# The first fifteen microseconds of a transformer layer: products of ones ahead of the first loads, x^T loaded in whole pairs, and a first contraction block in three rounds

## The chip, the cores and the metric

The kernel runs on one core of one Trainium2 chip. The metric is the device time in microseconds (us). The engines named here are TensorE (PE; its weight loads are shown as PEld), VectorE (DVE), ScalarE (ACT), GpSimd (POOL) and SyncE (SP), which issues nearly all loads and stores.

## The reference, cut to what matters

One layer over 1024 tokens of width 1024: two groups of attention heads side by side, cross-attention into 256 memory tokens, and a squared-ReLU MLP, each wrapped in RMSNorm. The change touches only the very first step, the input projection of the normalised x, and of it the values of the forgetting-attention heads:

```python
h = rmsnorm(x, g_mix_pre[l])
proj = h @ w_in[l]
fq = proj[..., 0:512]; fk = proj[..., 512:1024]; fv = proj[..., 1024:1536]
f_logit = proj[..., 1536:1544] + b_fgt[l]
...
x = x + rmsnorm(y @ w_out[l], g_mix_post[l])
...
x = x + rmsnorm(memory_cross_attention(...), g_mem_post[l])
...
x = x + rmsnorm(jnp.square(jax.nn.relu(h @ w_ff1[l])) @ w_ff2[l], g_ff_post[l])
```

All matrices are float32.

## The kernel before, in words

**Products.** A float32 product is made from three products in a faster form (fp32r): each operand is split into a high part (a rounded copy, made on ScalarE) and a low part (the rest, made on VectorE or GpSimd), and `mm3` (L172) issues high x high, high x low, low x high into the same PSUM bank. So no product can start before ScalarE has made the high parts of both operands, and the third waits for the low part of the activations.

**The opening (L1327 to L1495)** is written in the order in which it is to run; nothing is reordered by a planner there. It computes the values (`v`) of the forgetting heads for the first 512 tokens. x is not normalised first: x^T, scaled by the gain column `gp`, is split into `hT_hi` and `hT_lo` by `plain_split` (L1392, ScalarE at L1395, VectorE at L1396), and the row factor of the norm (`rall`, from squares of the rows of x) is applied when the banks are read out. The contraction over the 1024 features runs in eight blocks of 128 (kc = 0 to 7). `load_xt` (L1335) loads x^T in four pairs of blocks for each half of the tokens (tiles `xf`, 512 KB a pair), `load_wv` (L1341) loads the weights of the values (tiles `wv`; 264 columns in the first group, 256 in the second), and `wv_split` (L1374) makes `whiv` and `wlov` of them. The first pair and the first weight piece are cut in two, so that the first half pair (256 KB) and the weights of block 0 alone (132 KB) land first, and the two kinds are issued in turn (L1359):

```python
        for _ in zip(load_xt(0, 0, True), load_wv(0, 0, True)):
            pass
        list(load_xt(0, 1))
        list(load_wv(0, 1))
```

`value_part` (L1427) then goes block by block, and in a block bank by bank: four banks (128 tokens each), three products to a bank, 12 products of 264 columns to a block. Behind the 96 products of the first group come five blocks of the second group (60 products of 256 columns, needing low weights that GpSimd makes), then a small product `rt` (L1417) of a tile of ones with a diagonal of the row factors, then the other three blocks, and the same again for tokens 512 to 1023.

**Queues.** SP issues the loads one after the other, the gain column `gp` first (L1330). Each transfer signals on one of eight completion lanes in turn, and a transfer waits until the one eight places ahead of it has landed. ScalarE loads its table first, then waits for the weights of block 0. TensorE's first instruction is the first product of block 0. The constants (identity on GpSimd, two small columns and the tile `ones` on VectorE, L187 to L194) are written at the start; `ones` serves the products `rt`.

**The rest** (about 1420 us: attention, cross-attention and MLP) is recorded by a planner from estimated costs, which start at fixed numbers behind the opening and take no account of what stands in it.

Of the kernel before, what the change touches and what calls it, by code (L numbers as in the profile page):

```python
# [14 lines left out]
F32 = mybir.dt.float32  # L15
# [7 lines left out]
P = 128  # L23
S = 1024
D = 1024
KC = D // P
# [102 lines left out]
def layer(tc, out, t):  # L129
    nc = tc.nc  # L130
    ctx = ExitStack()
    with ctx:
        build(ctx, tc, nc, out, t)


def build(ctx, tc, nc, out, t):
    def pool(name, bufs=1, space=None, stack=ctx, **kw):
        if space is not None:
            kw["space"] = space
        return stack.enter_context(tc.tile_pool(name=name, bufs=bufs, reuse_waits="tile", **kw))  # L140

    const = pool("const")
# [7 lines left out]
    def mm_tile(shape, name, tag="mm"):  # L150
        return psp.tile(shape, F32, tag=tag, bufs=2, name=name)

    def u4(name, shape, dt=F32R):

        return up.tile(list(shape), dt, tag="u4", bufs=31, name=name)
# [16 lines left out]
    def mm3(ps, lh, ll, rh, rl, start, stop, more=False):  # L172

        nc.tensor.matmul(ps, lh, rh, start=start, stop=False, skip_group_check=more)  # L174
        nc.tensor.matmul(ps, lh, rl, start=False, stop=False, skip_group_check=more)  # L175
        nc.tensor.matmul(ps, ll, rh, start=False, stop=stop, skip_group_check=more)  # L176

    def rstd_of(ss, name):
# [5 lines left out]
        nc.gpsimd.tensor_tensor(r, r, mhalf[:, 0:1], op=ALU.pow)  # L184
        return r

    ident = const.tile([P, P], F32, name="ident")  # L187
    make_identity(nc, ident)
    mhalf = const.tile([P, 4], F32, name="mhalf")
    nc.vector.memset(mhalf, -0.5)  # L190
    o512 = const.tile([P, 1], F32, name="o512")
    nc.vector.memset(o512, 1.0 / 512.0)
    ones = const.tile([P, P], F32, name="ones")
    nc.vector.memset(ones, 1.0)  # L194
    bfgt = const.tile([P, 8], F32, name="bfgt")
    gcol = const.tile([P, KC], F32, name="gcol")
    gp = const.tile([P, KC], F32, name="gp")
# [1129 lines left out]
    stock = Stock()  # L1327
    back = Back()
    with tc.manual_schedule():
        nc.sync.dma_start(gp, t["g_pre"])  # L1330
        xf = [[None] * 4 for _ in range(2)]
        WV = ((0, 3), (3, 6), (6, 8)), ((0, 4), (4, 8))
        vraw = [[None] * 3, [None] * 2]

        def load_xt(th, kp, cut=False):  # L1335
            tag, n = (("klo", 4), ("sp", 5))[th]
            xf[th][kp] = p1.tile([P, 2, HT], F32, tag=tag, bufs=n, name=f"xf{th}{kp}")
            for c in (slice(0, 1), slice(1, 2)) if cut else (slice(0, 2),):
                yield nc.sync.dma_start(xf[th][kp][:, c, :], t["x_t"][th, kp][:, c, :])

        def load_wv(g, i, cut=False):  # L1341
            a, b = WV[g][i]
            shape = [P, b - a, 264 if g == 0 else 256]
            r = wp.tile(shape, F32, tag="wraw", bufs=3, name=f"wv{g}{i}") if g == 0 else u4(f"wv{g}{i}", shape, F32)
            vraw[g][i] = r
            for c in (slice(0, 1), slice(1, b - a)) if cut else (slice(0, b - a),):
                yield nc.sync.dma_start(r[:, c, :], t[f"w_v{g}"][:, a + c.start:a + c.stop, :])
# [8 lines left out]
            nc.sync.dma_start(r, t["x"][b * P:(b + 1) * P, :])  # L1356
            xrow.append(r)

        for _ in zip(load_xt(0, 0, True), load_wv(0, 0, True)):  # L1359
            pass  # L1360
        list(load_xt(0, 1))
        list(load_wv(0, 1))
        list(load_xt(0, 2))
        list(load_wv(0, 2))
        list(load_xt(0, 3))
        for i in range(2):
            list(load_wv(1, i))
        for b in range(4):
            load_row(b)
        for kp in range(4):  # L1370
            list(load_xt(1, kp))
        vs = [[u4(f"vs{g}_{i}", (P, 2, 4, P)) for i in range(4)] for g in range(2)]

        def wv_split(g, i, eng, cut=False):  # L1374
            raw = vraw[g][i]
            if g == 0:
                w = [u4(f"{m}v{g}{i}", raw.shape) for m in ("whi", "wlo")]
            else:
                w = [wp.tile(list(raw.shape), F32R, tag=m, bufs=2, name=f"{m}v{g}{i}") for m in ("whi", "wlo")]
            n = raw.shape[1]  # L1380

            def part(c):
                nc.scalar.activation(w[0][:, c, :], raw[:, c, :], AF.Copy)
                eng.tensor_sub(w[1][:, c, :], raw[:, c, :], f(w[0][:, c, :]))

            part(slice(0, 1 if cut else n))
            both = [(w[0][:, j, :], w[1][:, j, :]) for j in range(n)]
            return (both, lambda: part(slice(1, n))) if cut else both

        hT = [Act(f"hT{h}") for h in range(2)]  # L1390
# [31 lines left out]
        def value_banks(g, th):  # L1422
            tags = (("mm", "s"), ("tr", "pv"))[g]
            n = 264 if g == 0 else 256
            return [mm_tile([P, n], f"v{g}{th}{b}", tags[b // 2]) for b in range(4)]

        def value_part(banks, th, w, kcs):  # L1427
            for kc in kcs:
                for b in range(4):
                    c = slice(b * P, (b + 1) * P)  # L1430
                    mm3(banks[b], hT[th].hi(kc, c), hT[th].lo(kc, c), *w[kc], kc == 0, kc == KC - 1)
# [13 lines left out]
        w0, rest = wv_split(0, 0, nc.vector, True)  # L1445
# [8 lines left out]
        for kc in range(6, 8):  # L1454
            plain_split(0, kc)
        V = value_banks(0, 0)
        value_part(V, 0, w0, range(KC))
        w1 = wv_split(1, 0, nc.gpsimd)
        w1 += wv_split(1, 1, nc.gpsimd)
        for b in range(4):  # L1460
# [5 lines left out]
        stock.load(3)  # L1466
        W = value_banks(1, 0)
        value_part(W, 0, w1, range(5))
        d = root(0)
        values_out(0, 0, V)  # L1470
        spread(0, d, "s")
        value_part(W, 0, w1, range(5, 8))
        for kc in range(4):
            plain_split(1, kc)
        V = value_banks(0, 1)
# [64 lines left out]
    banks = [0]  # L1540

    def bank(name, tag=None):
        if tag is None:
            tag = ("mm", "s", "tr", "pv")[banks[0] % 4]
            banks[0] += 1
        return mm_tile([P, HT], name, tag)
# [54 lines left out]
    def first_row(j, wa, tags=(None, None)):  # L1601

        x = bank(f"px{j}", tags[0])
        product(x, wa, 0, B11)
        yb = bank(f"py{j}", tags[1])
        product(yb, wa, HT, B21)
        p1 = t2(f"p1_{j}")
        nc.scalar.activation(p1, x, AF.Copy)
        g11 = t2(f"g11_{j}")
        return x, p1, g11, lambda: nc.vector.tensor_add(g11, yb, p1)  # L1610
# [22 lines left out]
    xf = {}  # L1633
# [87 lines left out]
    for b in range(4):  # L1721
        c = slice(b * P, (b + 1) * P)
# [176 lines left out]
    with manual:  # L1899
        sums = lambda: None  # L1900
        for j in range(NP):
            more = j + 1 < NP
            after = Weights(j + 2) if j + 2 < NP else None
            w = cur.w
# [7 lines left out]
            if j < AHEAD:  # L1912
                p1, g11 = saved.pop(j)
                x = bank(f"px{j}")
            else:
                x, _, g11, add = first_row(j, w["a"])
# [156 lines left out]
        for n in range(7):  # L2073
# [4 lines left out]
            banks = Y if n in (1, 3, 5) else X  # L2078
# [87 lines left out]
```

## Time and profile before

| | |
|---|---|
| time, median of 3 runs | 1477.57 us (1474.86 to 1479.61) |
| time of the profiled execution | 1475.31 us |
| its span | 1473.5 us |
| PE busy | 1453.8 us (99%) |
| first product of block 0 | starts at 5.34 us |
| first product of block 1 | starts at 9.62 us |
| first product of the second group | starts at 22.11 us |

The span runs from the first instruction to the last in the profile; 1.8 us of the execution's own time lie around it. In the rows of the timeline the first number is the start in us from the start of the span, the second the duration; then engine, line, operation, output <- inputs, shape and count; in brackets stands the idle time before it and what ended that. Matmuls overlap in the rows: what one costs in a stream is the distance of the starts, not its duration.

### The profile page before, as it was taken

The numbers are of one execution on the slowest core, as the hardware profiler recorded it, in microseconds if no ns is written. First come the engines' busy times: TensorE is split into PE (matmuls) and PEld (weight loads), VectorE is DVE, ScalarE is ACT, GpSimd is POOL, SyncE is SP. The second block draws the span as 40 slices with busy tenths as digits, with TensorE's granted clock in tenths as the row PEclk, the third lists the DMA queues.
The fourth block names the chain that finished last, engine by engine and source line by source line (L and its number), as shares of the span: only waits on it lengthen the run. The fifth ranks groups of instructions, "written<-read, shape, count | busy, mean of one in ns | idle before, by whom it ended". The sixth has DMA issues, their size and how long they took to land. (4 is left out here: it accounts for less than half of the span.)

```text
span 1473.5 us, 20806 instructions
## 1 busy us (share of the span) xinstructions
PE 1453.8 (99%) x7260; PEld 1225.4 (83%) x7260; DVE 931.9 (63%) x1598; ACT 793.7 (54%) x1402; POOL 398.2 (27%) x488
## 2 busy tenths in 40 slices
PE   8999999999999999999999999999999999999998
PEld 7988888888889887888888887888888788888886
DVE  4467877667666545874474687765555666645577
ACT  6557776567577653554353455555555453444442
POOL 1335556444344201421121413342322000000021
PEclk9999999999999999999999999999999999999999
DMA  8234545635536677551341537764445785445565
GB/s 330 63 83 108 140 108 124 186 93 132 133 94 186 181 243 265 176 182 58 106 152 43 184 131 252 244 226 154 148 149 171 263 336 173 142 146 197 182 246 200
DMA packets 101753, 247.90 MB, mean 168 GB/s; under 512 B 12152, under 2 KB 24576, under 8 KB 101648
## 3 DMA queue, kind: packets, MB, share of 16 engines
q1 hardware_dynamic: 97040, 238.18, 48.5%
q0 software_dynamic: 4608, 8.39, 4.2%
q8 instruction: 57, 0.93, 0.3%
q14 instruction: 48, 0.39, 0.1%
HBM read 174.64 MB, written 71.88 MB: 167 GB/s over the span
## 5 line engine op out<-in xcount | busy, mean ns | idle before, releaser
L578 DVE TENSOR_TENSOR p<-ptr,p 128x512 fp32r<-128x512 f32 (+1 forms) x152 | 92.3, 616 | 40.9 <-ACT p L581 40.0
L1890 ACT ACTIVATE whif<-ra 128x1024 fp32r<-128x1024 f32 x37 | 39.2, 1061 | 122.7 <-PE fy L175 62.6
L1892 DVE TENSOR_TENSOR wlof<-ra,whif 128x1024 fp32r<-128x1024 f32 x37 | 45.3, 1225 | 91.7 <-ACT whif L1890 91.6
L581 ACT ACTIVATE p<-ptr 128x512 fp32r<-128x512 f32 (+1 forms) x152 | 79.6, 538 | 43.8 <-PE ptr L572 43.3
L2006 POOL TENSOR_SCALAR rf<-sf 128x1 f32<-128x1 f32 x8 | 8.2, 1031 | 326.7 <-ACT jf L1991 326.4
L622 PE MATMUL pv<-p,vs 128*128 128x512 f32 (+1 forms) x304 | 87.2, 373 | 1.7 <-DVE p L578 1.7
L174 PE MATMUL fx<-vhif,whif 128*128 128x512 f32 x168 | 65.4, 389 | 0.0
L175 PE MATMUL fx<-vlof,whif 128*128 128x512 f32 x168 | 65.4, 389 | 0.0
L176 PE MATMUL fx<-vhif,wlof 128*128 128x512 f32 x168 | 65.4, 389 | 0.0
L622 PEld LDWEIGHTS pv<-p,vs 128*128 128x128 f32 x304 | 53.4, 189 | 11.9 <-DVE p L578 3.5
L1780 POOL TENSOR_TENSOR sc<-wf,wf 128x512 f32<-128x512 f32 x14 | 22.4, 1597 | 142.7 <-DMA wf<-in_w_ff 134.7
L174 PE MATMUL k<-hT_hi,whik 128*128 128x512 f32 x128 | 52.7, 411 | 0.0
L174 PE MATMUL mq<-h2T_hi,whimq 128*128 128x512 f32 x128 | 51.6, 403 | 0.0
L174 PE MATMUL q<-hT_hi,whiq 128*128 128x512 f32 x128 | 51.1, 399 | 0.0
L174 PE MATMUL yw<-whiwo,yT_hi 128*128 128x512 f32 x128 | 50.8, 397 | 0.0
L631 ACT ACTIVATE ot<-pv 128x512 f32<-128x512 f32 x64 | 37.8, 591 | 23.5 <-PE pv L622 23.4
L174 PE MATMUL ym<-whimo,oT_hi 128*128 128x512 f32 x128 | 50.3, 394 | 0.1
L175 PE MATMUL k<-hT_lo,whik 128*128 128x512 f32 x128 | 50.2, 392 | 0.0
L176 PE MATMUL k<-hT_hi,wlok 128*128 128x512 f32 x128 | 50.2, 392 | 0.0
L175 PE MATMUL q<-hT_lo,whiq 128*128 128x512 f32 x128 | 50.1, 391 | 0.0
L175 PE MATMUL mq<-h2T_lo,whimq 128*128 128x512 f32 x128 | 50.0, 391 | 0.0
L176 PE MATMUL q<-hT_hi,wloq 128*128 128x512 f32 x128 | 50.0, 391 | 0.0
(592 smaller groups left out, 4928.5 us busy)
## 6 DMA issues: line engine op xcount, KB each, us to landing
ra<-gd SPq DMA_DIRECT2D x56, 512.0 KB, 3.8
wg<-in_w_ff SPq DMA_DIRECT2D x56, 512.0 KB, 5.1
wf<-in_w_ff SPq DMA_DIRECT2D x38, 512.0 KB, 3.8
gd<-s SPq DMA_DIRECT2D x48, 256.0 KB, 2.1
od<-ot SPq DMA_DIRECT2D x64, 128.0 KB, 2.4
od<-od POOLq DMA_DIRECT2D x32, 256.0 KB, 4.8
wrawmq<-in_w_mq SPq DMA_DIRECT2D x16, 512.0 KB, 4.1
wrawmo<-in_w_mo SPq DMA_DIRECT2D x16, 512.0 KB, 3.8
```

What stands on the lines that cost most here:

```text
L174: nc.tensor.matmul(ps, lh, rh, start=start, stop=False, skip_group_check=more)
L175: nc.tensor.matmul(ps, lh, rl, start=False, stop=False, skip_group_check=more)
L176: nc.tensor.matmul(ps, ll, rh, start=False, stop=stop, skip_group_check=more)
L578: flow.put("V", at, 0.56 if dead else 0.7, lambda: nc.vector.tensor_sub(pl[:, live, :], tr[:, live, :], f(ph[:, live, :])), done)
L581: flow.put("S", flow.end, 0.49 if dead else 0.6, lambda ph=ph, tr=tr, live=live: nc.scalar.activation(ph[:, live, :], tr[:, live, :], AF.C ...
L622: nc.tensor.matmul(pv[:, :, q0 * P:(q0 + k1 - k0) * P], v, x[:, :, k0:k1, :].rearrange("p m k q -> p m (k q)"), start=c == 0 and m == 0, s ...
L631: nc.scalar.activation(box["t"][:, :, :, ::step], pv.rearrange("p m (k q) -> p m k q", q=P), AF.Copy)
L1780: eng.tensor_sub(sc[:, k1], r0[:, k0], r1[:, k0])
L1890: nc.scalar.activation(ah, ra, AF.Copy)
L1892: nc.vector.tensor_sub(al, ra, f(ah))
L2006: nc.gpsimd.tensor_scalar(r, ssf[b][:, 0:1], ssf[b][:, 1:2], EPS, op0=ALU.add, op1=ALU.add)
```

## The change

- The tile `ones` is written first of all constants, so VectorE's first instruction is this memset.
- The gain column `gp` is loaded from ScalarE's queue, not from SP's.
- TensorE begins with seven plain float32 products of `ones` with `ones` (128 x 128 each) into a PSUM tile `warm` that nothing reads.
- The first pair of x^T is loaded as one transfer of 512 KB, not as two halves; the order of the first transfers is weights of block 0, first pair, rest of the first weight piece, and then as before.
- Block 0 runs in three rounds over the four banks: high x high for all four, then high x low weights for all four, then low x high for all four. Blocks 1 to 7 are as before.

```diff
@@ constants
+    ones = const.tile([P, P], F32, name="ones")
+    nc.vector.memset(ones, 1.0)
     ident = const.tile([P, P], F32, name="ident")
...
-    ones = const.tile([P, P], F32, name="ones")
-    nc.vector.memset(ones, 1.0)
@@ opening
-        nc.sync.dma_start(gp, t["g_pre"])
+        nc.scalar.dma_start(gp, t["g_pre"])
+        warm = mm_tile([P, P], "warm", "tr")
+        for _ in range(7):
+            nc.tensor.matmul(warm, ones, ones, start=True, stop=True)
...
-        def load_xt(th, kp, cut=False):
+        def load_xt(th, kp):
             tag, n = (("klo", 4), ("sp", 5))[th]
             xf[th][kp] = p1.tile([P, 2, HT], F32, tag=tag, bufs=n, name=f"xf{th}{kp}")
-            for c in (slice(0, 1), slice(1, 2)) if cut else (slice(0, 2),):
-                yield nc.sync.dma_start(xf[th][kp][:, c, :], t["x_t"][th, kp][:, c, :])
+            nc.sync.dma_start(xf[th][kp], t["x_t"][th, kp])
...
-        for _ in zip(load_xt(0, 0, True), load_wv(0, 0, True)):
-            pass
-        list(load_xt(0, 1))
+        first = load_wv(0, 0, True)
+        next(first)
+        load_xt(0, 0)
+        list(first)
+        load_xt(0, 1)
         list(load_wv(0, 1))
...
+        def value_first(banks, w):
+            hs, ls = ([x(0, slice(b * P, (b + 1) * P)) for b in range(4)] for x in (hT[0].hi, hT[0].lo))
+            for b in range(4):
+                nc.tensor.matmul(banks[b], hs[b], w[0], start=True, stop=False)
+            for b in range(4):
+                nc.tensor.matmul(banks[b], hs[b], w[1], start=False, stop=False)
+            for b in range(4):
+                nc.tensor.matmul(banks[b], ls[b], w[0], start=False, stop=False)
...
-        value_part(V, 0, w0, range(KC))
+        value_first(V, w0[0])
+        value_part(V, 0, w0, range(1, KC))
```

On TensorE's queue, at the very start of the program, the order before was this (`v` is a bank of the values, `hT_hi` and `hT_lo` the split x^T, `whiv` and `wlov` the split weights; in brackets the engine whose signal is waited for):

```order
L174 MATMUL v_230<-whiv_200,hT_hi_182 128x264 [waits Activation_49]
L175 MATMUL v_230<-wlov_201,hT_hi_182 128x264 [waits DVE_49]
L176 MATMUL v_230<-whiv_200,hT_lo_186 128x264 [waits DVE_49]
L174 MATMUL v_231<-whiv_200,hT_hi_182 128x264
L175 MATMUL v_231<-wlov_201,hT_hi_182 128x264
```

And with the change, at the same place:

```order
L1333 MATMUL warm<-ones 128x128 [waits DVE_49]
L1333 MATMUL warm<-ones 128x128 x6
L1434 MATMUL v_237<-whiv_207,hT_hi_189 128x264 [waits Activation_49]
L1434 MATMUL v_238<-whiv_207,hT_hi_189 128x264
L1434 MATMUL v_239<-whiv_207,hT_hi_189 128x264
L1434 MATMUL v_240<-whiv_207,hT_hi_189 128x264
L1436 MATMUL v_237<-wlov_208,hT_hi_189 128x264 [waits DVE_49]
L1436 MATMUL v_238<-wlov_208,hT_hi_189 128x264
L1436 MATMUL v_239<-wlov_208,hT_hi_189 128x264
L1436 MATMUL v_240<-wlov_208,hT_hi_189 128x264
L1438 MATMUL v_237<-whiv_207,hT_lo_193 128x264 [waits DVE_49]
```

The seven products stand in front of block 0 and wait for the memset alone; the wait for the low part of x^T moved from the third product of block 0 to the ninth.

SP's queue at the start of the program, before:

```order
L1330 DMA gp<-in_g_pre 128x8
L1339 DMA xf_138<-in_x_t 128x512
L1347 DMA wv_140<-in_w_v 128x264
L1339 DMA xf_138<-in_x_t 128x512
L1347 DMA wv_140<-in_w_v 128x528
L1339 DMA xf_144<-in_x_t 128x1024
L1347 DMA wv_146<-in_w_v 128x792
L1339 DMA xf_148<-in_x_t 128x1024
L1347 DMA wv_150<-in_w_v 128x528 [waits DMAHW0_49]
L1339 DMA xf_152<-in_x_t 128x1024 [waits DMAHW1_49]
```

And with the change (`DMAHW` are the eight completion lanes):

```order
L1349 DMA wv_146<-in_w_v 128x264
L1341 DMA xf_148<-in_x_t 128x1024
L1349 DMA wv_146<-in_w_v 128x528
L1341 DMA xf_151<-in_x_t 128x1024
L1349 DMA wv_153<-in_w_v 128x792
L1341 DMA xf_155<-in_x_t 128x1024
L1349 DMA wv_157<-in_w_v 128x528
L1341 DMA xf_159<-in_x_t 128x1024 [waits DMAHW0_49]
```

The weights of block 0 moved from the third place to the first and the rest of the first weight piece from the fifth to the third; everything behind stands two places earlier. `gp` still holds the first lane, now from ScalarE's queue, where it stands ahead of the table load. Behind block 0 the order of all five engines is the same in both kernels.

More of the change, by code (lines that the diff above doesn't have):

```diff
@@ L1357, in load_row @@
             xrow.append(r)
-        for _ in zip(load_xt(0, 0, True), load_wv(0, 0, True)):
-            pass
-        list(load_xt(0, 1))
+        first = load_wv(0, 0, True)
[3 more added lines that the diff above has]
+        load_xt(0, 1)
         list(load_wv(0, 1))
-        list(load_xt(0, 2))
+        load_xt(0, 2)
         list(load_wv(0, 2))
-        list(load_xt(0, 3))
+        load_xt(0, 3)
         for i in range(2):
@@ L1370, in build @@
         for kp in range(4):
-            list(load_xt(1, kp))
+            load_xt(1, kp)
         vs = [[u4(f"vs{g}_{i}", (P, 2, 4, P)) for i in range(4)] for g in range(2)]
```

## The prediction

> **What bounds the kernel now.** I read the page first, then the opening in the timeline, since the change touches nothing behind it.
>
> ```profile
> span 1473.5 us, 20806 instructions
> PE 1453.8 (99%) x7260; PEld 1225.4 (83%) x7260; DVE 931.9 (63%) x1598; ACT 793.7 (54%) x1402; POOL 398.2 (27%) x488
> ```
>
> TensorE bounds the whole: 19.7 us of the span are without a product. What the opening saves reaches the end if no load or side engine further on is late for an earlier TensorE. So the questions are how early TensorE's stream can run, and at what pace. Its start, products and ScalarE together:
>
> ```profile
> 0.73 1.28 ACT L1383 ACT_TABLE_LOAD   x1 [0.73 <-PEq L2159]
> 0.89 0.17 DVE L194 MEMSET ones<- 128x128 f32 x1
> 4.25 0.42 ACT L1383 ACTIVATE whiv<-wv 128x264 fp32r<-128x264 f32 x1 [2.25 <-DMA wv<-in_w_v]
> 4.58 0.71 ACT L1395 ACTIVATE hT_hi<-xf,gp 128x512 fp32r<-128x512 f32 x1
> 5.34 0.59 PE L174 MATMUL v<-whiv,hT_hi 128*128 128x264 f32 x1 [5.34 <-ACT hT_hi L1395]
> 6.13 0.59 PE L176 MATMUL v<-whiv,hT_lo 128*128 128x264 f32 x1
> 8.28 0.42 PE L176 MATMUL v<-whiv,hT_lo 128*128 128x264 f32 x1
> 8.31 0.64 ACT L1383 ACTIVATE whiv<-wv 128x528 fp32r<-128x528 f32 x1 [3.03 <-DMA wv<-in_w_v]
> 9.62 0.59 PE L174 MATMUL v<-whiv,hT_hi 128*128 128x264 f32 x1 [0.93 <-ACT hT_hi L1395]
> ```
>
> Block 0 runs from 5.34 to about 8.5 (last start 8.28 plus one distance). Block 1 waits until 9.62 for a load: the rest of the first weight piece comes at 8.3, ScalarE splits it, then x^T of block 1. So whatever block 0 saves on its own is spent waiting for block 1; only what moves 9.62, or the pace behind it, counts. The pace:
>
> ```profile
> 13.44 0.42 PE L174 MATMUL v<-whiv,hT_hi 128*128 128x264 f32 x1
> 13.66 0.42 PE L175 MATMUL v<-wlov,hT_hi 128*128 128x264 f32 x1
> 14.10 0.30 PE L174 MATMUL v<-whiv,hT_hi 128*128 128x264 f32 x1
> 14.48 0.28 PE L174 MATMUL v<-whiv,hT_hi 128*128 128x264 f32 x1
> 14.61 0.28 PE L175 MATMUL v<-wlov,hT_hi 128*128 128x264 f32 x1
> 22.11 0.28 PE L174 MATMUL v<-whiv,hT_hi 128*128 128x256 f32 x1
> ```
>
> Starts are 0.22 us apart up to 14.1 and 0.12 to 0.13 after it: TensorE ran at half pace until then (the granted-clock column still reads 1.00 there, so I go by the distances). From 9.62 to 14.10 stand 19 starts; at 0.12 they take 2.3 us, not 4.5. So the half pace costs at most 2.2 us behind 9.62. It ended after 4.5 us without an idle stretch; the 3.2 us of block 0, followed by 1.1 us idle, had not ended it. How fast it comes back shows at the kernel's end, where TensorE stops at about 1466.2:
>
> ```profile
> 1466.00:1468.00 2.00, 0.17 (x1) 0.00 (x0) 1.51 (x3) 0.72 (x2) 0.19 (x1) 1.00 0.68 262
> 1468.00:1470.00 2.00, 0.00 (x0) 0.00 (x0) 1.23 (x2) 0.00 (x0) 0.65 (x2) 0.55 0.00 0
> ```
>
> (Columns: busy time of PE, PEld, DVE, ACT, POOL, then granted clock, DMA share, GB/s.) A mean of 0.55 over 2 us means full clock for 0.2 us and half for the rest: the half clock is back at 1468.2, 2.0 us after the last product.
>
> **The change, part by part.** *Loads.* What SP issues first, and what the transfers reach:
>
> ```profile
> 0.73 0.39 SPq L1330 DMA_DIRECT2D gp<-in_g_pre  x1
> 1.17 0.42 SPq L1339 DMA_DIRECT2D xf<-in_x_t  x1
> 1.64 0.42 SPq L1347 DMA_DIRECT2D wv<-in_w_v  x1
> 2.58 0.43 SPq L1347 DMA_DIRECT2D wv<-in_w_v  x1
> 2.00:3.00 1.00, 0.00 (x0) 0.00 (x0) 0.00 (x0) 0.01 (x1) 0.00 (x0) 1.00 0.65 168
> 3.00:4.00 1.00, 0.00 (x0) 0.00 (x0) 0.00 (x0) 0.00 (x0) 0.00 (x0) 1.00 0.95 258
> 4.00:5.00 1.00, 0.00 (x0) 0.00 (x0) 0.29 (x1) 0.75 (x2) 0.00 (x0) 1.00 0.83 175
> 5.00:6.00 1.00, 0.66 (x2) 0.50 (x2) 0.82 (x2) 0.29 (x1) 0.00 (x0) 1.00 0.89 273
> 9.00:10.00 1.00, 0.38 (x1) 0.38 (x2) 1.00 (x2) 1.00 (x2) 0.00 (x0) 1.00 1.02 415
> ```
>
> SP issues one transfer per 0.47 us. Block 0's weights move from 1.64 to 0.73, the rest of that piece (block 1's) from 2.58 to 1.67, and everything behind stands 0.9 earlier, two issues fewer. The first bulk transfer is issued 0.44 earlier (1.17 to 0.73). That is the sure part; the other half of the 0.9 counts only where the DMA engines have room, and they are 65 to 95% busy from 2 us on. So block 1's data come between 0.44 and 0.92 earlier; I take 0.7, the middle, because neither end has a row nearer to it. If ready weights were no earlier at all, the term is 0. From 6 us on the loads are a stream at full rate, so the later ones shift by the same.
>
> `gp` on ScalarE's queue costs ScalarE one issue (0.39) ahead of the 1.28 table load: that ends at 2.4 instead of 2.0. ScalarE idles until 4.25 there, so it costs nothing; if the first weights land at 3.3 (2.6 after their issue, as before) 0.9 of cover is still left.
>
> *The whole first pair.* Block 0 now needs 512 + 132 KB instead of 256 + 132. The added 256 KB at 168 to 258 GB/s take 1.0 to 1.6 us, less the 0.44: x^T lands 0.6 to 1.2 later, around 4.9 to 5.5 if it was there at 4.3. First product at 5.9 to 6.5, not 5.34. Block 0 then takes 12 x 0.22 = 2.6 us at half pace and ends at 8.5 to 9.1. Block 1 is ready at 9.62 - 0.7 = 8.9. So this costs 0 to 0.2; the old wait ahead of block 1 is its cover.
>
> *Three rounds.* The two waits inside block 0 (its first three products take 1.18 us from 5.34 to 6.52, where three distances are 0.66) go, 0.5 us. Again in the shadow of block 1: worth nothing.
>
> *Memset.* `ones` first on VectorE: 0.17 us, the other two columns 0.17 later, used much later. Nothing.
>
> *Seven products of ones.* Their price is not in the trace of before. The nearest row is the `rt` product, also plain float32 and with ones as an operand, 512 columns, recorded as two instructions:
>
> ```profile
> 29.30 1.02 PE L1417 MATMUL rt<-diag,ones 128*128 128x512 f32 x2
> 16.05 4.88 POOL L1384 TENSOR_TENSOR wlov<-wv,whiv 128x1024 fp32r<-128x1024 f32 x2 [14.76 <-ACT whiv L1383]
> 23.89 0.87 DVE L1412 TENSOR_SCALAR diag<-ident,rall 128x128 f32<-128x128 f32 x4 [7.59 <-POOL rall L1409]
> 12.29 2.07 DVE L1396 SCALAR_TENSOR_TENSOR hT_lo<-xf,gp,hT_hi 128x512 fp32r<-128x512 f32 x3
> ```
>
> A quarter of its columns is 0.26 at full pace, 0.5 at half, so seven take 3.6 us, from about 1.1 (memset at 0.80 + 0.17, plus the signal) to 4.7. Upper end: if weight loads don't overlap, 14 instructions of 0.29 + 0.26 take 7.7 us and end at 8.8. They add nothing to TensorE's path as long as they end before 5.9; beyond that block 0 is pushed back.
>
> What they buy is pace. Busy stretches become 1.1 to 4.7 and 5.9 to 8.5, against 5.3 to 8.5 before. If the half pace ends in there and stays ended, block 1 on runs at 0.12. Its data allow nearly that: 12 products take 1.44 us, and the low parts of blocks 3 to 5 (12.29, three in 2.07) come 0.7 apart; block 3's is ready at 13.0 where the faster stream would use it at 12.74 (9.62 + 2 x 1.44 + 0.24), a wait of 0.3. So the gain behind block 1 is at most 2.2 - 0.3 = 1.9. The lower end is a full pace that comes no earlier relative to block 1: 0. I take 1.6, nearer the upper end: 6 us of work in the 7.4 us ahead of block 1 is more than the 3.2 in 4.3 that did not do it.
>
> [...]
>
> *Who is late next.* With 2.3 us gained the second group starts at 19.8 instead of 22.11. It needs GpSimd's first low weights, half of 4.88 after 16.05, so 18.5, itself moved earlier with its load. The `rt` product moves from 29.30 to 27.0; its diagonal is ready at 24.76. No wait. Behind it everything is relative to TensorE.
>
> **Sum.** 0.7 (loads) + 1.6 (pace) = 2.3 us off the profiled 1475.31, which gives 1473.0. The median of the runs lies 2.26 above the profiled execution; 2.3 off 1477.57 gives 1475.3, my forecast.
>
> **Rivals.** (1) *The products of ones don't change the pace.* They stop at 4.7, x^T comes at 5.9; the gap of over a second breaks the activity, as the 1.1 us gap did before. Then only the loads' 0.7 stays: 1476.9. For it speaks that 3.2 us did not suffice; against it that 3.6 and 2.6 us stand close together.
>
> (2) *The load start speeds up too.* From 2 to 6 us the loads moved 0.87 MB (168 + 258 + 175 + 273 GB/s), at the later 415 it would be 1.66 MB: 1.9 us are lost there. If whole pairs in longer rows cure that, block 1 comes 1.9 + 0.44 earlier, and with the pace 1.9: 4.2 us, 1473.3. Against it: the change only merges two of the first six transfers.
>
> (3) *Slower: the whole pair lands late.* All later loads share the engines with it, and a pair issued among seven others took 7.8 us:
>
> ```profile
> xf<-in_x_t SPq DMA_DIRECT2D x1, 512.0 KB, 7.8
> ```
>
> It decides once block 0 would end after 9.62 at half pace: landing + 0.71 + 2.64 > 9.62, a landing after 6.3, which is 5.1 after its issue at 1.2. At 7.8 it lands at 9.0, block 0 starts at 9.7 and ends at 12.3 with block 1 waiting behind: 2.7 us lost, 1480.3. Against it: the half pair took under 3.1 us (issue 1.17, in use at 4.58).
>
> **Chances.** The forecast 0.50; (1) 0.25; (2) 0.15; (3) 0.10. The forecast's own range is 1473.5 to 1477, from 0.5 to 4 us of gain, since the windows of the pace and 2 to 3 us of spread between runs are in it. The range for 8 in 10 goes from 1471.5 (case 2 and a low run) to 1479.2 (a third of the way into case 3, and a high run of no gain). About 0.3%, 4.4 us, is what a measurement of this kernel can tell from no change: faster means under 1473.1, slower over 1482.0. Under 1473.1 lie about half of (2) and a fifth of the forecast: 0.18. Over 1482.0 lies only a bad (3) in a high run: 0.06. Within: 0.76.
>
> **What would show it.** Right: seven products from about 1.1 to 4.7; the rest of the first weight piece split by ScalarE at about 7.6; block 1 at about 8.9; starts 0.12 apart from there on; the second group at about 19.8; `rt` at about 27.0, with no wait of TensorE ahead of it. Rival 1: starts 0.22 apart until after 12. Rival 2: over 350 GB/s from 3 us on. Rival 3: ScalarE waits for x^T past 6.3. The forecast is wrong if a place behind the opening changes by itself, or if the wait between blocks 0 and 1 brings the half pace back.

## The result

Over 14 runs of each kernel side by side the median went from 1474.88 us (1472.13 to 1479.61) to 1471.43 us (1469.61 to 1475.03). The ratio is 0.9978, with a 95% interval of 0.9969 to 0.9987: 3.2 us faster, between 1.9 and 4.6. The forecast was a gain of 2.3 from a median of 1477.57; the longer row of runs puts the kernel before 2.7 lower than the three runs did, and the time after lies 0.07 below the range stated for 8 in 10, and 2.1 below the forecast's own 1473.5 to 1477, for that reason. The gain itself was forecast 0.9 too small; it lies inside the 0.5 to 4 us that the forecast's own range stood for.

The page of the kernel after, and its opening in the timeline (columns as before: start, duration, engine, line, operation):

```profile
span 1467.8 us, 20832 instructions
PE 1453.2 (99%) x7274; PEld 1225.7 (84%) x7274; DVE 929.8 (63%) x1598; ACT 794.1 (54%) x1402; POOL 401.7 (27%) x488
```

```profile
1.05 3.35 PE L1333 MATMUL warm<-ones 128*128 128x128 f32 x14 [1.05 <-DVE o L194]
3.13 0.42 ACT L1387 ACTIVATE whiv<-wv 128x264 fp32r<-128x264 f32 x1 [0.69 <-DMA wv<-in_w_v]
4.89 0.72 ACT L1399 ACTIVATE hT_hi<-xf,gp 128x512 fp32r<-128x512 f32 x1 [1.33 <-DMA xf<-in_x_t]
5.52 0.63 ACT L1387 ACTIVATE whiv<-wv 128x528 fp32r<-128x528 f32 x1
5.66 0.76 PE L1434 MATMUL v<-whiv,hT_hi 128*128 128x264 f32 x4 [1.26 <-ACT hT_hi L1399]
7.23 0.29 PE L174 MATMUL v<-whiv,hT_hi 128*128 128x264 f32 x1
7.35 0.28 PE L175 MATMUL v<-wlov,hT_hi 128*128 128x264 f32 x1
7.73 0.39 PE L176 MATMUL v<-whiv,hT_lo 128*128 128x264 f32 x1
8.97 0.87 ACT L1387 ACTIVATE whiv<-wv 128x792 fp32r<-128x792 f32 x1 [0.32 <-DMA wv<-in_w_v]
9.17 0.28 PE L175 MATMUL v<-wlov,hT_hi 128*128 128x264 f32 x1
9.49 0.39 PE L176 MATMUL v<-whiv,hT_lo 128*128 128x264 f32 x1
10.92 0.37 PE L175 MATMUL v<-wlov,hT_hi 128*128 128x264 f32 x1
11.57 0.39 PE L176 MATMUL v<-whiv,hT_lo 128*128 128x264 f32 x1 [0.27 <-DVE hT_lo L1400]
18.69 0.28 PE L174 MATMUL v<-whiv,hT_hi 128*128 128x256 f32 x1
25.88 1.02 PE L1421 MATMUL rt<-diag,ones 128*128 128x512 f32 x2
```

The weights of blocks 3 to 5 were split in the kernel before at:

```profile
10.49 0.86 ACT L1383 ACTIVATE whiv<-wv 128x792 fp32r<-128x792 f32 x1 [0.26 <-DMA wv<-in_w_v]
```

The seven products of ones last from 1.05 to 4.40, and the full pace is there from block 0 on (four products from 5.66 in 0.76). The rest of the first weight piece, for which block 1 had waited until 8.31, is split at 5.52 with no wait for its load at all, 2.8 earlier; the weights of blocks 3 to 5 are split only 1.5 earlier (8.97). Block 1 starts at 7.23 instead of 9.62, the second group at 18.69 instead of 22.11, the `rt` product at 25.88 instead of 29.30. From there the two timelines run 3.4 to 3.5 us apart as far as 430 us. TensorE now waits inside blocks 1 to 3 for low parts of x^T (the products at 7.73, 9.49 and 11.57 start 0.38, 0.32 and 0.65 after the one ahead of them instead of 0.12): about 1 us. The last of these waits, at 11.57, ends a chain through ScalarE and VectorE that begins with the load of the weights of blocks 3 to 5 (8.97); behind it TensorE runs without a wait to the second group.

The loads by stages of 1 us (busy time of PE, PEld, DVE, ACT, POOL, then granted clock, DMA share, GB/s):

```profile
2.00:3.00 1.00, 1.00 (x7) 1.00 (x6) 0.00 (x0) 0.44 (x1) 0.00 (x0) 1.00 1.00 265
3.00:4.00 1.00, 1.00 (x7) 1.00 (x6) 0.41 (x1) 0.42 (x1) 0.00 (x0) 1.00 0.93 361
4.00:5.00 1.00, 0.40 (x2) 0.11 (x1) 0.02 (x1) 0.11 (x1) 0.00 (x0) 1.00 1.04 331
5.00:6.00 1.00, 0.34 (x2) 0.34 (x3) 0.36 (x1) 1.00 (x2) 0.00 (x0) 1.00 0.92 287
```

From 2 to 6 us the loads moved 1.24 MB, against 0.87 before.

The spans of the two profiled executions differ by 5.7 us, more than the medians. The 2.3 behind 430 us are not shown to be part of the change: TensorE's order is the same there, and three waits in each profile between 430 and 580 us, 2.6 us together before and 1.1 after, make 1.5 of it. They are, before and then after (engine, line and what it waited for: us, times, longest):

```profile
PE ptr L572 <- POOL spc6g L515: 1.1, 1, 1.1
PE pv L622 <- DVE p L578: 1.0, 1, 1.0
PE mv L174 <- ACT whimv L311: 0.5, 1, 0.5
```

```profile
PE sc6g L499 <- DVE mnc6g L503: 0.4, 1, 0.4
PE pv L622 <- DVE p L578: 0.4, 1, 0.4
PE mv L174 <- ACT whimv L311: 0.3, 1, 0.3
```

Such waits differ between two profiles of one and the same program: TensorE's idle time from 555 to 562 us, where the last one falls, was 1.05 in this profile of the changed kernel and 1.83 in its repetition (experiment 7).

### The profile page after: what moved, and what is told of

Same layout as the page of the kernel before. It is cut to its first block, busy times and chain, and to the rows that moved or that the text cites. A ratio compares the mean times of both kernels' runs of the same rounds, so it can differ in the third digit from the quotient of the medians.

```text
span 1467.8 us, 20832 instructions
## 1 busy us (share of the span) xinstructions
PE 1453.2 (99%) x7274; PEld 1225.7 (84%) x7274; DVE 929.8 (63%) x1598; ACT 794.1 (54%) x1402; POOL 401.7 (27%) x488
```

## The experiments

Theory at this point: the gain is made of earlier loads, which start block 1 earlier, and of the earlier full pace. Rivals: the loads alone, since the faster stream meets its data anyway; the ones alone; and luck of one run with the first loads. This table gathers what the profiles of all kernels show, so that the parts below need not repeat it; all times in us from the start of the span, read from the timelines as above ("rest split": when ScalarE starts on the rest of the first weight piece; "full pace": from when starts are 0.12 apart).

| kernel | x^T split | rest split | block 0 | block 1 | full pace | second group |
|---|---|---|---|---|---|---|
| before | 4.58 | 8.31 | 5.34 | 9.62 | 14.1 | 22.11 |
| after | 4.89 | 5.52 | 5.66 | 7.23 | from block 0 | 18.69 |
| after, once more | 5.08 | 5.71 | 5.85 | 8.66 | 8.8 | 18.88 |
| no ones | 5.12 | 5.75 | 5.90 | 8.71 | 11.2 | 20.01 |
| old loads | 4.51 | 8.07 | 5.28 | 9.38 | 13.5 | 21.68 |
| gain column on SP | 5.59 | 6.22 | 6.37 | 8.43 | from block 0, lost 7.3 to 10.7 | 19.62 |
| pair in halves, 2 KB rows | 3.83 | 7.32 | 4.60 | 8.62 | in block 0, lost 8.7 to 12 | 20.63 |
| pair in halves, 4 KB rows | 6.35 | 6.97 | 7.12 | 9.93 | 12.0 | 21.04 |
| pair ahead of the weights | 5.05 | 7.25 | 5.81 | 8.61 | 8.8 | 19.38 |
| no rounds | 5.63 | 6.26 | 6.41 | 9.56 | 12.3 | 20.98 |
| twelve ones | 4.90 | 5.55 | 5.68 | 7.23 | from block 0 | 18.69 |
| twelve ones, no rounds | 5.46 | 6.08 | 6.23 | 8.33 | from block 0 | 18.53 |
| twelve ones, all rounds | 5.04 | 5.67 | 5.82 | 7.38 | from block 0 | 17.95 |
| the same, and low weights last in mv | 5.37 | 6.00 | 6.19 | 7.73 | from block 0 | 17.99 |

**1. Without the products of ones.**

```diff
-        warm = mm_tile([P, P], "warm", "tr")
-        for _ in range(7):
-            nc.tensor.matmul(warm, ones, ones, start=True, stop=True)
```

> The changed kernel without the seven products of ones; loads and rounds as changed. Theory P (pace and loads both count): block 1 starts at about 7.5 to 8.5, its products stand 0.22 apart until a stretch of some 4 us without idle time has passed (until 10 to 13 us), the second group starts 1 to 2.2 us later than in the changed kernel (18.69), at 19.7 to 20.9; time between the two kernels. Theory L (the loads alone carry the gain, TensorE catches up with the data anyway): second group at 18.7 to 19.2. Theory O (the ones carry it all): second group at about 22.

The ratio to the kernel before is 0.9983 (0.9970 to 0.9997). In the profile the loads are as early as after the change, the pace is not; the products around its change:

```profile
10.91 0.42 PE L175 MATMUL v<-wlov,hT_hi 128*128 128x264 f32 x1
11.13 0.33 PE L176 MATMUL v<-whiv,hT_lo 128*128 128x264 f32 x1
11.30 0.28 PE L174 MATMUL v<-whiv,hT_hi 128*128 128x264 f32 x1
20.01 0.28 PE L174 MATMUL v<-whiv,hT_hi 128*128 128x256 f32 x1
```

Second group at 20.01: of the 3.4 us of the changed profile 2.1 came without any product of ones, 1.3 did not. That is what P expected (its block 1, at 8.71, came 0.2 past the 8.5: with block 0 at half pace it starts when block 0 is through; the half pace ended 5.3 us behind the start of block 0, with no idle time in between). It is one profile of each kernel, and the 2.1 hold more than earlier data: the half pace ended at 11.2 there and at 14.1 in the kernel before, where TensorE stood idle for about 1 us between blocks 0 and 1; here it did not. In the times the difference to the changed kernel is not resolved (0.9983 against 0.9978, intervals that overlap).

**2. The loads as before, ones and rounds kept.**

```diff
-        nc.scalar.dma_start(gp, t["g_pre"])
+        nc.sync.dma_start(gp, t["g_pre"])
...
-        first = load_wv(0, 0, True)
-        next(first)
-        load_xt(0, 0)
-        list(first)
+        first = load_wv(0, 0, True)
+        load_xt(0, 0)
+        for c, _ in zip((slice(0, 1), slice(1, 2)), range(2)):
+            nc.sync.dma_start(xf[0][0][:, c, :], t["x_t"][0, 0][:, c, :])
+            next(first)
```

(`load_xt` issues nothing for the first pair here.)

> The seven products of ones and the three rounds kept; gain column on SP first and the first pair in two halves in turn with the weights, as before. Theory P: block 1 back at about 9.6, products 0.12 apart if the full pace outlasts the idle time between blocks 0 and 1 (some 2.5 us), second group at 19.9 to 20.5 (the 1.9 us of the prediction's pace term gained, the rest lost). If the half pace comes back in that idle time: starts 0.22 apart again after 9.6 and second group at 21 to 22. Theory L: second group at about 22. Theory V (the early start of block 1 in the changed profile was one run's luck with the first loads): block 1 starts anywhere between 7 and 10 whatever the order of the loads.

The ratio is 1.0001 (0.9985 to 1.0016): no gain in the time. The profile:

```profile
1.05 3.35 PE L1333 MATMUL warm<-ones 128*128 128x128 f32 x14 [1.05 <-DVE o L194]
5.28 1.25 PE L1436 MATMUL v<-whiv,hT_hi 128*128 128x264 f32 x4 [0.87 <-ACT hT_hi L1401]
8.07 0.64 ACT L1389 ACTIVATE whiv<-wv 128x528 fp32r<-128x528 f32 x1 [2.85 <-DMA wv<-in_w_v]
9.38 0.59 PE L174 MATMUL v<-whiv,hT_hi 128*128 128x264 f32 x1 [1.10 <-ACT hT_hi L1401]
13.42 0.33 PE L175 MATMUL v<-wlov,hT_hi 128*128 128x264 f32 x1
21.68 0.28 PE L174 MATMUL v<-whiv,hT_hi 128*128 128x256 f32 x1
```

ScalarE waits for the rest of the piece until 8.07, as before the change; so the early loads are the work of the change and not luck, and V falls: the split comes at 8.07 and 8.31 in the two profiles with the old loads, and at 5.52 to 6.26 in the eight with the changed ones (one of them with another edit far behind). And although the seven products ran, block 0 ran at half pace (1.25 for four products), and the full pace came only at 13.5: the ones did nothing in this run. The expectation had taken the full pace in block 0 for granted; that was wrong. So this profile does not show what an early full pace would be worth with the old loads; the time says only that seven products of ones bring no gain there that is resolved, and twelve were not tried with them.

**3. The gain column first on SP's queue, the rest as changed.**

```diff
-        nc.scalar.dma_start(gp, t["g_pre"])
+        nc.sync.dma_start(gp, t["g_pre"])
```

> The changed kernel with the gain column first on SP's queue again, so that all bulk loads are issued 0.45 us later. If the issue time counts: block 0's and block 1's loads and the second group 0.4 to 0.5 us later (19.1 to 19.2). If the 128 short rows ahead of the bulk loads slow the start of the stream: the DMA rate from 2 to 5 us falls back to about 200 GB/s and block 1 starts at 9 or later.

x^T is split 0.70 later than in the changed profile, and the rest of the piece too. That lies within what the same loads vary by from run to run (x^T at 4.89 to 5.63 in the profiles with the changed loads); the first weights show the later issue more clearly:

```profile
3.45 0.42 ACT L1387 ACTIVATE whiv<-wv 128x264 fp32r<-128x264 f32 x1 [1.44 <-DMA wv<-in_w_v]
```

In the profiles with the changed loads this split comes at 2.88 to 3.13. From 2 to 5 us the loads move 261 GB/s on average, against 319 in the changed kernel and the 200 of the second expectation; block 1 starts at 8.43, not at 9 or later. Four microseconds shifted by the issue time, from 2.45 on, have 300, against 311 from 2 on in the changed kernel, which leaves little for the short rows. But the second group comes 0.9 later, not 0.4 to 0.5. The stages show why:

```profile
6.00:7.00 1.00, 0.63 (x5) 0.64 (x6) 0.65 (x1) 1.00 (x3) 0.00 (x0) 1.00 0.95 376
7.00:8.00 1.00, 1.00 (x9) 1.00 (x8) 1.00 (x3) 0.47 (x1) 0.00 (x0) 0.65 0.99 336
10.00:11.00 1.00, 1.00 (x7) 1.00 (x7) 0.55 (x1) 1.00 (x3) 0.00 (x0) 0.64 1.04 415
```

The granted clock falls to half 0.3 into the stage from 7 to 8 (mean 0.65) and comes back 0.72 into the stage from 10 to 11 (mean 0.64): 3.42 us of half pace, while TensorE was working. In the same length of time before 7.30 it had worked only to 4.21 and again from 6.37: 1.26 of 3.42, or 37%.

**4. The first pair in two halves of 256 KB with rows of 2 KB.**

```diff
-            nc.sync.dma_start(xf[th][kp], t["x_t"][th, kp])
+            for c in (slice(0, 1), slice(1, 2)) if th + kp == 0 else (slice(0, 2),):
+                nc.sync.dma_start(xf[th][kp][:, c, :], t["x_t"][th, kp][:, c, :])
```

> The changed kernel with the first pair of x^T as two transfers of 256 KB behind one another (rows of 2 KB), the rest as changed. If the longer rows cure the slow start (rival 2): the rate from 2 to 6 us falls to about 220 GB/s and block 1 starts at 8.5 to 9.5. If the order and the earlier issue carry it: rate and block 1 (7.2) within 0.5 us of the changed kernel, and block 0 starts up to 0.8 earlier than 5.66.

```profile
4.60 1.04 PE L1435 MATMUL v<-whiv,hT_hi 128*128 128x264 f32 x4 [0.20 <-ACT hT_hi L1400]
7.32 0.64 ACT L1388 ACTIVATE whiv<-wv 128x528 fp32r<-128x528 f32 x1 [2.77 <-DMA wv<-in_w_v]
8.62 0.57 PE L174 MATMUL v<-whiv,hT_hi 128*128 128x264 f32 x1 [2.01 <-ACT hT_hi L1400]
```

Block 0 starts 1.06 earlier than in the changed kernel, and block 1 later by 1.4, since the rest of the weights now comes at 7.32. From 2 to 6 us the loads move 267 GB/s, between the 219 of the kernel before and the 311 of the changed one. The time gained ahead of block 0 is lost ahead of block 1, and behind the idle stretch of 2 us between them the pace is half again from 8.7 to 12 (mean granted clock 0.84 from 8 to 9, 0.50 from 9 to 12, 0.96 from 12 to 13). A good part of the loads' gain hangs on the whole pair.

**5. The pair in two transfers cut by partitions, so that the rows keep 4 KB.**

```diff
-            nc.sync.dma_start(xf[th][kp], t["x_t"][th, kp])
+            for c in (slice(0, 64), slice(64, 128)) if th + kp == 0 else (slice(0, 128),):
+                nc.sync.dma_start(xf[th][kp][c, :, :], t["x_t"][th, kp][c, :, :])
```

> The changed kernel with the first pair of x^T in two transfers again, but cut by partitions: 64 partitions each, so that the rows keep their 4 KB. In the two halves with rows of 2 KB the rest of the first weight piece was split at 7.32 instead of 5.52. If the row length does it: split at about 5.5 to 6, block 1 at about 7.2 to 7.7. If the number of transfers does it: split at about 7.3, block 1 at about 8.6.

```profile
6.35 0.72 ACT L1400 ACTIVATE hT_hi<-xf,gp 128x512 fp32r<-128x512 f32 x1 [2.96 <-DMA xf<-in_x_t]
```

Neither of the two came: x^T itself lands late (split at 6.35 after 2.96 us of waiting; block 1 at 9.93), and the rest of the piece is ready when ScalarE gets to it at 6.97. The long rows alone do not give the early start.

**6. The whole pair ahead of block 0's weights.**

```diff
         first = load_wv(0, 0, True)
-        next(first)
         load_xt(0, 0)
+        next(first)
         list(first)
```

> The changed kernel with the whole first pair ahead of block 0's weights. If only the whole pair and the early issue count, and not the order: the rest of the piece is split at 5.3 to 6 as in the changed kernel and block 0 starts at 5.3 to 5.9, the weights of block 0 being split at 4 or later. If the order counts: block 0 or 1 more than 0.5 us later.

```profile
7.25 0.64 ACT L1387 ACTIVATE whiv<-wv 128x528 fp32r<-128x528 f32 x1 [1.50 <-DMA wv<-in_w_v]
```

The order counts: x^T comes as in the changed kernel, but ScalarE waits for the rest of the piece until 7.25. (Block 1, at 8.61, says nothing of the loads: block 0 ran at half pace and was through only then, as in the next experiment.) So the early loads need two things together, one transfer for the pair and the small weights ahead of it; the earlier issue adds its own half microsecond (the first weights split at 3.45 without it, at 2.88 to 3.13 with it). Each was taken back in one profile only: without the one transfer or the order, x^T or the rest of the piece is split 1.5 to 1.8 us later. Why a small transfer behind the pair, or a cut of the pair, delays the next by so much is not explained by these runs.

**7. The changed kernel once more, unchanged.**

> The changed kernel once more, unchanged. [...] Theory V (luck with the loads): the rest of the piece at 7 or later.

```profile
5.85 1.25 PE L1434 MATMUL v<-whiv,hT_hi 128*128 128x264 f32 x4 [1.45 <-ACT hT_hi L1399]
8.66 0.36 PE L174 MATMUL v<-whiv,hT_hi 128*128 128x264 f32 x1
8.86 0.28 PE L175 MATMUL v<-wlov,hT_hi 128*128 128x264 f32 x1
18.88 0.28 PE L174 MATMUL v<-whiv,hT_hi 128*128 128x256 f32 x1
```

The same program, with the loads as in the first profile (the rest of the piece split at 5.71, so V falls here too), and this time block 0 ran at half pace up to 8.8; block 1 came at 8.66 instead of 7.23 for that reason alone. Yet the second group came only 0.19 later than in the first profile: block 1 started 1.43 later and then did not have to wait for the low parts. Ahead of some 9 us the full pace is worth next to nothing with these loads, because the weights of blocks 3 to 5 are not there (split at 8.97 and 9.05 in the two profiles).

**8. Twelve products of ones.** (`range(7)` becomes `range(12)`.)

> The changed kernel with twelve products of ones instead of seven. They last from 1.05 to 5.4 to 6.8, so that TensorE has no idle time ahead of block 0. [...] Theory N (the products of ones have no steady effect): time as the changed kernel. If they overrun: block 0 starts after 6.4, second group at 19.5 or later, time above the changed kernel.

They end at 5.84, block 0 starts at 5.68 by the modelled ends, with no idle time, and the opening is that of the best profile (18.69). The time is no better than with seven: 0.9986 (0.9976 to 0.9995). So N is right on the time, although the pace was full from block 0 on in all four profiles with twelve products. The profile shows one thing that can hide a gain, at 500 and 565 us:

```profile
498.00:500.00 2.00, 0.26 (x1) 0.26 (x2) 1.68 (x3) 2.00 (x5) 0.00 (x0) 0.97 0.09 30
502.00:504.00 2.00, 2.00 (x9) 1.68 (x8) 0.88 (x2) 0.80 (x2) 0.00 (x0) 0.68 0.88 146
562.00:564.00 2.00, 0.58 (x2) 0.27 (x2) 1.23 (x1) 1.67 (x2) 0.00 (x0) 1.00 0.17 64
564.00:566.00 2.00, 2.00 (x7) 1.58 (x8) 1.98 (x2) 1.28 (x2) 0.00 (x0) 0.68 0.51 111
568.00:570.00 2.00, 2.00 (x10) 1.56 (x10) 1.12 (x1) 1.28 (x2) 0.00 (x0) 0.96 0.75 231
```

Twice TensorE waits for some 1.8 us, the second time in two pieces (it was busy 0.26 and 0.58 of the 2 us shown), and the half clock comes from 499.9 to 503.3 and from 564.7 to 568.2, some 1.7 us lost each time (mean granted clock 0.50 from 500 to 502 and from 566 to 568). In the changed kernel's first profile neither happened. But that does not by itself explain why no gain shows: the runs with a mean granted clock of 0.999, the highest on record, have a median of 1470.41 with twelve products (3 of 11 runs) and of 1470.35 with seven (7 of 14).

**9. Twelve products, and rounds in all eight blocks.**

```diff
-        value_first(V, w0[0])
-        value_part(V, 0, w0, range(1, KC))
+        value_rounds(V, range(KC))
```

(`value_rounds` is `value_first` for every block of the list, starting the banks in the first and closing them in the last.)

> Twelve products of ones, and all eight blocks of the first group in three rounds over the four banks, so that the low parts are needed 0.7 to 1 us later within a block. Theory: in the changed kernel TensorE waits about 1 us in blocks 1 to 3 for low parts (products at 7.73, 9.49, 11.57); these waits go, second group at 17.7 to 18.6, time 1 to 2 us below the changed kernel. If the high parts and loads are what binds: second group as with twelve products alone.

The waits for low parts go: the second group starts at 17.95, 0.74 earlier. The time, 0.9982 (0.9973 to 0.9991), can't be told from the changed kernel's; the 1 to 2 us that were expected did not come.

**10. Block 0 bank by bank, once with seven and once with twelve products.**

```diff
-        value_first(V, w0[0])
-        value_part(V, 0, w0, range(1, KC))
+        value_part(V, 0, w0, range(KC))
```

> The changed kernel with block 0 bank by bank as before (no rounds). If the rounds are worth nothing, as predicted: second group where the pace of this run puts it (18.7 at full pace from the start, 19.6 to 20 otherwise). If block 1 follows block 0 without a wait, block 0's wait for the low part (0.5 us) shows in the second group.

> Twelve products of ones, so that the pace is full from block 0 on, and block 0 bank by bank. Worth nothing, as predicted: second group at 18.7 as with twelve and rounds. If block 1 now stands close behind block 0: block 0's first low part is waited for in the third product, some 0.4 to 0.6 us, and the second group comes 0 to 0.6 later, the less since blocks 1 to 3 wait for their low parts anyway.

With seven, x^T came 0.74 later than in the first profile and the full pace only at 12.3, so 20.98 tells nothing of the rounds. With twelve the wait inside block 0 is there (its third product waits for the low part until 7.02, 0.56 behind the second), and the second group still comes at 18.53, against 18.69 with rounds. The weights of blocks 3 to 5 were split 0.17 earlier in that profile (8.80), which is about the whole difference. So no worth of the rounds shows, in one profile of each.

**11. Low weights last in the memory values, on top of 9.**

```diff
+                    kcs = (kp * 2, kp * 2 + 1)
-                    for j in range(2):
-                        kc = kp * 2 + j
-                        mm3(ps[m], mT.hi(kc, ms), mT.lo(kc, ms), wh[:, j, :], wl[:, j, :], kc == 0, kc == KC - 1)
+                    for j, kc in enumerate(kcs):
+                        nc.tensor.matmul(ps[m], mT.hi(kc, ms), wh[:, j, :], start=kc == 0, stop=False)
+                        nc.tensor.matmul(ps[m], mT.lo(kc, ms), wh[:, j, :], start=False, stop=False)
+                    for j, kc in enumerate(kcs):
+                        nc.tensor.matmul(ps[m], mT.hi(kc, ms), wl[:, j, :], start=False, stop=kc == KC - 1)
```

> Twelve products of ones and rounds in all eight blocks, and one more edit far behind the opening: in the memory values (products mv) the two products with the high weights come first and those with the low weights last, since TensorE waits there about 0.3 us for the high and 0.8 us for the low part of the last weight block in every profile, and in three profiles the half pace came back for 3.4 us behind that wait. Theory: the wait of 0.8 goes, the half pace comes back there in fewer runs; time 0.8 to 1.8 us below the kernel without this edit, ratio to the kernel before 0.9970 or lower. If the load or the high part is what binds: no change.

The wait of 0.8 for the low weights goes; the only wait of TensorE in that stretch that is left is for the high part:

```profile
PE mv L880 <- ACT whimv L311: 0.8, 1, 0.8
```

The time does not show it: 0.9982 (0.9969 to 0.9994), where 0.9970 or lower was expected. That the high part, which waits for its load, is what binds then is what this profile suggests; it was not tested by itself. No version of these is shown to beat the changed kernel.

## Why the prediction was right, and where it was off

- **What bounds the opening** held in part. Block 0's own savings are worth nothing: no worth of the rounds shows (10.), and block 0 starts later as foretold (5.66 to 6.41 in the profiles with the changed loads and the ones in front, against 5.9 to 6.5). But with the early loads block 1 no longer waits for its data; it follows block 0, at 7.23 where the pace is full and at 8.66 and 8.71 where it is half (7. and 1.). And block 1 isn't what counts then: its 1.43 between the first profile and the repetition moved the second group by 0.19. The weights of blocks 3 to 5 come next, through the wait at 11.57; with rounds in all blocks, which take that wait away, the second group comes 0.74 earlier (9.).
- **The loads' term is the step that failed.** It was bounded by the issue times, "between 0.44 and 0.92 earlier", and taken as 0.7. Block 1's weights were there 2.8 us earlier (5.52 instead of 8.31). Block 1 itself started 2.4 earlier, part of it by the full pace in block 0. Without the ones, these loads moved the second group by 2.1, an earlier end of the half pace included. The bound was too narrow: an earlier issue was not all that the edit changed, the stream of the first loads became denser (1.24 instead of 0.87 MB from 2 to 6 us). Nor did "the later ones shift by the same" hold: the lead was 2.8 at the first weight piece and 1.5 at the second. That the start of the loads speeds up was the second rival's mechanism, given 0.15. Its condition of over 350 GB/s from 3 us on was met only from 3 to 4; its load term of 1.9 + 0.44 = 2.3 is near what came, and its price of 4.2 us was too high because the pace's 1.9 did not come on top. The loads are what carries the gain: with the old loads the ratio is 1.0001 (0.9985 to 1.0016, which just touches the 0.9969 to 0.9987 of the change), without the ones 0.9983.
- **The pace term** was taken as 1.6, at most 1.9. Measured by taking the ones away it is 1.3 in one profile, and in the times nothing that is resolved. The cap was worked out with the data where they were; the stream that starts earlier meets them, and TensorE waits about 1 us in blocks 1 to 3. It also left out block 0, whose pace had no worth as long as block 1 waited for its load. Of eight profiles with seven products of ones the full pace was there ahead of or in block 0 in three, and in two of these it was lost again; with twelve it was there in four of four and stayed through the opening. The forecast's range rests on "the windows of the pace" too: no run shows such windows; what the runs showed is that the full pace came ahead of block 0 in one profile of the changed kernel and at 8.8 in the other.
- **Luck**: by experiment 1 the loads were put 1.4 too low and the pace 0.3 too high, errors of opposite sign, and the range for 8 in 10 was 7.7 us wide. That the seven products brought the full pace ahead of block 0 in the first profile is chance too, as the repetition shows.
- **What the prediction warned of** came: "if the wait between blocks 0 and 1 brings the half pace back" happened with the halves, and in the wait ahead of block 0 with the gain column on SP. The idle stretches were 2.0 us in the one (experiment 4, granted clock 0.50 from 9 to 12) and 2.2 us in the other (experiment 3, 0.50 from 8 to 10); behind the 1.26 us ahead of block 0 in the first changed profile the pace was full.
- **The products of ones** ran from 1.05 to 4.40, 3.35 us for seven; 3.6, to 4.7, was foretold from the `rt` row.
- **Who is late next**: the diagonal for `rt` was ready in time (24.29, for a product at 25.88), and up to 430 us nothing behind the opening changed by itself, as the sum assumed; behind that the waits vary from run to run, as said above. (In rival 1, "the gap of over a second" is one of over a microsecond.) That rival 1 gives "only the loads' 0.7" was wrong with the same term.

## What to carry to other kernels

At the start of a program, look for the load that the second piece of work waits for, not the first: here the first product began 0.3 us later, and the gain came from the weights of block 1 and of those behind it. When that wait is gone, look for the next load that is late: here the weights of blocks 3 to 5. Bound what an edit of the first loads may do by what the loads could move at their later rate, not by the issue times alone (here 1.66 MB from 2 to 6 us at 415 GB/s; 0.87 moved before and 1.24 after). Ask whether the data will be there when TensorE is fast: here keeping it busy ahead of them was worth 1.3 us in one profile (experiment 1), and with the pace full from block 0 on the second group came only 0.19 earlier than in the repetition at half pace up to 8.8 (18.69 and 18.88). And a microsecond disappears in the differences from run to run (1469.61 to 1475.03 for one kernel) unless the runs are many.

## What the runs showed of the hardware that was not expected

The half clock, once it was back, lasted nearly the same each time: 3.42 us in experiment 3 (from 7.30 on) and 3.4 us twice in experiment 8 (from 499.9 and from 564.7 on), with TensorE at work. In the same length of time before it set in, TensorE had worked 37% of the time in experiment 3 and 44% and 51% in experiment 8; in the 3.4 us before the full pace came at 8.8 in experiment 7 it had worked 87% (from 5.85 on). These shares come from these few profiles alone; what decides the pace they do not show. Whether seven products of ones bring the full pace early changed from profile to profile: in three profiles of one and the same loads it began before 5.66, at 8.8 and, without rounds, at 12.3.
